# Linear attention on one core: Q of eight groups in 8 KB runs, with transposes and outputs taken by pairs of groups

## The chip, the cores and the metric

The kernel runs on one core of a Trainium2 chip. The metric is the device time of one execution in microseconds (us); lower is better. Each kernel was run several times beside the kernel before on the same chip. A ratio is the mean time of one kernel's fast runs over the mean of the other's fast runs of the same rounds, so it is not quite the ratio of the medians that are quoted. A run is called slow here when it lies more than 1.5% above the fastest run of the same kernel. With one core there is no second die to compare with, and for the changed kernel this limit cuts through one broad scatter (132.4 to 136.5 us), whose cause is looked at below.

The diffs are shortened, and some comments in them are not in the kernels. "Full" and "half clock" are read from the PEclk row of the profile (9 or 5 tenths granted) and from the times: the same 32 matmuls took 2.34 us and 4.48 us. PSUM is the memory in which the kernel keeps TensorE's results, SBUF the one for everything else on the chip that it works on.

The engines are TensorE (PE in the profile; PEld is its weight load), VectorE (DVE), ScalarE (ACT), GpSimd (POOL, which here issues most transfers) and SyncE (SP, which issues five).

## The reference

```python
batch, heads, seq, dim = 8, 12, 512, 64          # Q, K, V: float32
Q_feat = np.maximum(0, Q) + 1
K_feat = np.maximum(0, K) + 1
KV = np.einsum('bhkd,bhkv->bhdv', K_feat, V)
K_sum = np.sum(K_feat, axis=2)
numerator = np.einsum('bhqd,bhdv->bhqv', Q_feat, KV)
denominator = np.einsum('bhqd,bhd->bhq', Q_feat, K_sum)
return numerator / (denominator[:, :, :, None] + 1e-10)
```

Each of the 96 heads has 512 rows of 64. The three inputs are 37.7 MB and the output is 12.6 MB.

## The kernel before

The work is cut into 12 groups of 8 heads, two quads of four heads each. Pairs of groups share a load. A load casts fp32 to bf16 on its way. For each group VectorE makes the features of K and Q and spreads three quarters of V into a block layout (ScalarE the fourth); TensorE multiplies keys by values (`keys_values`), ScalarE brings the result (`kva`) from PSUM to SBUF; TensorE transposes Q's features into PSUM, ScalarE copies them out as `qt`; TensorE multiplies `qt` by `kva` (`output`), and VectorE divides out of PSUM into `o_sb`, which is stored. In the timelines of these runs each engine takes its instructions in the order of the program's calls: in group 9 of the changed kernel, output products that were ready began only at 97.45, when the transposes called before them were done.

```python
psum_qt = ctx.enter_context(tc.tile_pool(name="psum_qt", bufs=2, space=bass.MemoryType.PSUM))
...
def load(s, groups, names="kvq"):                  # 4 KB runs of fp32 per partition
    ...
        nc.gpsimd.dma_start(out=t[:, ms], in_=drams[x][:, 2 * groups[0] : 2 * groups[-1] + 2])

def load_pair(s):
    if s < NG // 2 - 1:
        load(s, (2 * s, 2 * s + 1))
    else:                                          # the last pair: by group
        load(s, (2 * s,))
        load(s, (2 * s + 1,))

def transposes(g):
    qf = qfs.pop(g)
    qt = mid_pool.tile([P, C, P, 2], BF16, name="qt")
    for half in range(2):
        qt_ps = psum_qt.tile([P, C, P], BF16, name="qt_ps")
        for c in range(C):
            nc.tensor.transpose(qt_ps[:, c, :], qf[:, half * C + c, :, :], identity)
        nc.scalar.copy(out=qt[:, :, :, half], in_=qt_ps)
    qts[g] = qt
...
for g in range(NG - 1):
    k_features(g)
    v_blocks(g)
    q_features(g)
    if g:
        transposes(g - 1)
    if g >= 2:
        output(g - 2)
    keys_values(g)
    if g % 2 and g // 2 + 2 < NG // 2:
        load_pair(g // 2 + 2)
    if g >= LAG:
        store(g - LAG)
last = NG - 1
k_features(last)
v_blocks(last)
transposes(last - 1)
output(last - 2)
q_features(last)
keys_values(last)
transposes(last)
output(last - 1)
output(last)
...
```

## Time and profile before

| | before |
|---|---|
| median of the first 3 runs | 127.46 us |
| span in the profile | 125.8 us |
| DMA | busy nine tenths or more in every slice from the second to the last but one |
| VectorE | 70% busy; its last instruction ends at 120.36 |
| VectorE idle ahead of reciprocals (first instruction of each output eviction) | 4.9 us in all |
| keys-by-values products, 32 matmuls of a group | 2.34 us at full clock, up to 4.48 at half |

The page of the profile has the span in 40 slices of some 3.1 us; a digit is the busy share in tenths, and the GB/s row counts a casting load by the bf16 that it writes, so 210 there is 420 of fp32 read. The groups list, for instructions of one line and tile, the busy time and the mean in ns, and behind the second bar how long the engine was idle ahead of them and what ended most of that. This is the row that the argument turns on, for the kernel before:

```profile
L199 DVE RECIPROCAL recip<-o_ps 128x8 f32<-128x8 f32 x48 | 9.6, 199 | 4.9 <-PE o_ps L189 4.8
```

VectorE waits for output products 4.8 us in the whole kernel.

### The profile page before, as it was taken

What the parts mean: (1) busy time and instruction counts of PE and PEld (TensorE: products, weight loads), DVE (VectorE), ACT (ScalarE), POOL (GpSimd) and SP (SyncE); (2) the same over time, 40 slices, a digit from 0 to 9 for tenths busy, and PEclk for the clock granted to TensorE, in tenths of its full rate; (3) what the DMA queues carried; (4) which work ended last, traced back from release to release, by engine and by line L of the source; (5) the groups of instructions that cost most, each with busy time, mean ns of one, the idle gap of its engine ahead of it and who ended that gap; (6) DMA issues with size and microseconds to landing.
All of it is one profiled execution on the core that took longest, in us unless ns stands there. A gap on an engine that the chain in (4) does not pass through costs nothing.

```text
span 125.8 us, 2337 instructions
## 1 busy us (share of the span) xinstructions
PE 65.2 (52%) x960; PEld 48.4 (39%) x960; DVE 88.2 (70%) x188; ACT 68.0 (54%) x87; POOL 27.8 (22%) x43
## 2 busy tenths in 40 slices
PE   0005939000059784796918476006978569694500
PEld 0003627000036564574806365004656447472300
DVE  4896280206199799999989990629959999758920
ACT  7832296006700889629892962750087971987000
POOL 6990213000002082023700260212221002020000
PEclk9999999755555999689999999955589976999955
DMA  3999999999999999999999999999999999999991
GB/s 76 341 211 209 210 213 211 210 212 211 212 211 212 211 214 212 210 212 214 253 414 287 209 210 212 213 369 380 209 210 210 211 287 418 418 417 410 403 391 72
DMA packets 13419, 32.13 MB, mean 255 GB/s; under 512 B 608, under 2 KB 608, under 8 KB 13408
## 3 DMA queue, kind: packets, MB, share of 16 engines
q0 software_dynamic: 12048, 28.84, 98.3%
q1 hardware_dynamic: 1360, 3.15, 6.8%
q8 instruction: 7, 0.11, 0.3%
q14 instruction: 4, 0.03, 0.1%
HBM read 37.75 MB, written 12.58 MB: 400 GB/s over the span
## 4 chain that ended last, share of the span: by engine, by line
DMA 40%; DVE 26%; PE 18%; POOL 6%; issue 6%; DVEq 0%; POOLq 0%
DMA q_raw<-in_Q_dram 40%; DVE o_sb L200 15%; PE kva_ps L157 11%; DVE v_all L140 4%; PE qt_ps L176 3%; DVE recip L199 3%; PE o_ps L189 3%; POOL v_raw L99 2%; DVE qf L122 2%; DVE kf L122 2%; POOL q_raw L99 1%; POOL kva_diag L231 1%; POOL k_raw L99 1%; POOL identity masks.py:199 0%; POOL identity masks.py:197 0%
## 5 line engine op out<-in xcount | busy, mean ns | idle before, releaser
L157 PE MATMUL kva_ps<-v_all,kf 128*64 128x320 bf16 x384 | 36.4, 356 | 13.1 <-DVE v_all L140 13.1
L189 PE MATMUL o_ps<-kva_diag,qt 128*64 128x130 bf16 x384 | 19.1, 234 | 40.9 <-DVE o_sb L200 40.4
L200 DVE TENSOR_TENSOR o_sb<-o_ps,recip 128x512 f32<-128x512 f32 x48 | 33.2, 692 | 1.6
L140 DVE COPY v_all<-v_raw 32x2048 bf16<-32x2048 bf16 x36 | 26.5, 736 | 10.9 <-DMA v_raw<-in_V_dram 10.6
L157 PEld LDWEIGHTS <-kf 128*64 128x64 bf16 x384 | 25.3, 133 | 20.9 <-DVE v_all L140 13.3
L189 PEld LDWEIGHTS <-qt 128*64 128x64 bf16 x384 | 12.7, 114 | 46.4 <-DVE o_sb L200 44.6
L138 ACT COPY v_all<-v_raw 32x2048 bf16<-32x2048 bf16 x12 | 22.7, 1894 | 13.3 <-DMA v_raw<-in_V_dram 13.1
L177 ACT COPY qt<-qt_ps 128x1024 bf16<-128x1024 bf16 x24 | 29.7, 1308 | 0.3
L167 ACT CAST kva_diag<-kva_ps 64x256 bf16<-64x256 f32 x24 | 8.9, 371 | 33.3 <-PE kva_ps L157 33.2
L122 DVE TENSOR_SCALAR qf<-q_raw 128x1024 bf16<-128x1024 bf16 x24 | 9.1, 423 | 6.6 <-DMA q_raw<-in_Q_dram 6.5
L99 POOL DMA_DIRECT2D k_raw<-in_K_dram x7 | 5.3, 754 | 38.1 <-DVE kf L122 37.3
L116 POOL DMA_DIRECT2D out_dram<-o_sb x10 | 8.4, 846 | 22.6 <-DVE o_sb L200 16.4
L176 PE MATMUL qt_ps<-identity,qf 128*128 128x128 bf16 x192 | 13.1, 222 | 0.0
L199 DVE RECIPROCAL recip<-o_ps 128x8 f32<-128x8 f32 x48 | 9.6, 199 | 4.9 <-PE o_ps L189 4.8
L122 DVE TENSOR_SCALAR kf<-k_raw 128x1024 bf16<-128x1024 bf16 x22 | 8.7, 437 | 6.0 <-DMA k_raw<-in_K_dram 6.0
L176 PEld LDWEIGHTS <-qf 128*128 128x128 bf16 x192 | 11.0, 99 | 3.3 <-issue 3.0
L99 POOL DMA_DIRECT2D v_raw<-in_V_dram x8 | 6.1, 764 | 18.8 <-ACT v_all L138 10.7
L99 POOL DMA_DIRECT2D q_raw<-in_Q_dram x8 | 5.9, 741 | 4.2 <-DMA q_raw<-in_Q_dram 4.2
L213 DVE MEMSET v_all<- 128x3072 f32 (+1 forms) x2 | 4.4, 2192 | 1.1 <-DVE ones L225 0.7
L168 ACT CAST kva_diag<-kva_ps 64x4 bf16<-64x4 f32 x24 | 4.0, 169 | 0.0
L214 ACT COPY v_all<-zero 128x2048 f32<-128x2048 f32 x2 | 3.7, 1894 | 0.0
L214 ACT ACT_TABLE_LOAD x1 | 1.3, 1283 | 0.7 <-PEq L273 0.7
(12 smaller groups left out, 4.6 us busy)
## 6 DMA issues: line engine op xcount, KB each, us to landing
out_dram<-o_sb POOLq DMA_DIRECT2D x10, 1024.0 KB, 20.2
k_raw<-in_K_dram POOLq DMA_DIRECT2D x4, 1024.0 KB, 18.0
v_raw<-in_V_dram POOLq DMA_DIRECT2D x4, 1024.0 KB, 20.9
q_raw<-in_Q_dram POOLq DMA_DIRECT2D x4, 1024.0 KB, 25.0
v_raw<-in_V_dram POOLq DMA_DIRECT2D x4, 512.0 KB, 17.3
q_raw<-in_Q_dram POOLq DMA_DIRECT2D x4, 512.0 KB, 17.1
out_dram<-o_sb SPq DMA_DIRECT2D x4, 512.0 KB, 5.1
k_raw<-in_K_dram POOLq DMA_DIRECT2D x3, 512.0 KB, 23.3
```

The source lines that it names most:

```text
L99: nc.gpsimd.dma_start(out=t[:, ms], in_=drams[x][:, 2 * groups[0] : 2 * groups[-1] + 2])
L116: nc.gpsimd.dma_start(out=o_to, in_=o_sb)
L122: nc.vector.tensor_scalar(out=dst, in0=src, scalar1=1.0, scalar2=1.0, op0=ALU.add, op1=ALU.max)
L138: nc.scalar.copy(out=v_blk[g % 2][ps, b], in_=v_raw[ps])
L140: nc.vector.tensor_copy(out=v_blk[g % 2][ps, b], in_=v_raw[ps])
L157: nc.tensor.matmul(kva_ps[64 * n : 64 * n + 64], lhsT=kf[:, c, n, :], rhs=vb[:, :, n, c, :], start=(c == 0), stop=(c == C2 - 1),)
L167: nc.scalar.copy(out=kva[ps, :, n, 0:D], in_=kva_ps[ps, sb : sb + 4, :])
L176: nc.tensor.transpose(qt_ps[:, c, :], qf[:, half * C + c, :, :], identity)
L177: nc.scalar.copy(out=qt[:, :, :, half], in_=qt_ps)
L189: nc.tensor.matmul(ops[c // 4][64 * j : 64 * j + 64, c // 2 % 2, (c % 2) * W : (c % 2) * W + W], lhsT=qt[:, c, 32 * b : 32 * b + 32, :], r ...
L199: nc.vector.reciprocal(out=recip, in_=cells[:, :, :, :, D:D1])
L200: nc.vector.tensor_tensor(out=o_sb[:, h:NP:2, 4 * i : 4 * i + 4].rearrange("p n (b c) d -> p b c n d", b=2), in0=cells[:, :, :, :, 0:D], i ...
```

## The change

Groups 2 to 9 read Q in 8 KB runs of fp32 per partition instead of 4 KB (a load is of sixteen heads in both kernels). A partition then holds rows of both groups' heads in another order, so a group's transposes give `qt` for parts of both groups, the outputs of a pair need the `qt` and the `kva` of both, and the transposes of a pair are made together. The store of each group goes to every second pair of heads. Two things come along: K and V of the last pair are one load each instead of one by group, and the calls at the end stand in another order. The idea is that longer runs cost the transfers less.

```diff
+    def eights(g):
+        return 2 <= g < NG - 2
+    def load_q(s):
+        t = in_pool.tile([P, 4, C2, D], BF16, name="q_raw").rearrange(
+            "p (n r) (q c) d -> p n (r q c) d", n=2, c=C)
+        nc.gpsimd.dma_start(out=t, in_=q_eights[:, 2 * s : 2 * s + 2])
     ...
     def load_pair(s):
-        if s < NG // 2 - 1:
-            load(s, (2 * s, 2 * s + 1))
-        else:
-            load(s, (2 * s,))
-            load(s, (2 * s + 1,))
+        pair = (2 * s, 2 * s + 1)
+        load("k", pair)
+        load("v", pair)
+        if eights(2 * s):
+            load_q(s)
+        else:
+            for g in pair:
+                load("q", (g,))
     ...
     def transposes(g):
-            nc.scalar.copy(out=qt[:, :, :, half], in_=qt_ps)
+            nc.scalar.copy(
+                out=qts[g][:, lo : lo + CC // 2], in_=qt_ps.rearrange("p c r q -> p c q r"))
     ...
     def output(g):
+                    if eights(g):
+                        b = 2 * (g % 2) + j
+                        kva = kva_diag[(g // 2 * 2 + h) % NV]        # NV: 4 instead of 3
+                        q = slice(16 * (4 * h + b), 16 * (4 * h + b) + 16)
     ...
-        for g in range(NG - 1):
+        for g in range(last):
             k_features(g)
             v_blocks(g)
-            q_features(g)
-            if g:
+            if not eights(g) and g < last - 1:
+                q_features(g)
+            if eights(g) and g % 2:
+                transposes(g - 1)
+                transposes(g)
+            elif g and not eights(g - 1):
                 transposes(g - 1)
             if g >= 2:
                 output(g - 2)
+            if eights(g) and g % 2 == 0:
+                q_features(g)
+                q_features(g + 1)
             keys_values(g)
     ...
         k_features(last)
         v_blocks(last)
+        output(last - 2)
+        keys_values(last)
+        q_features(last - 1)
         transposes(last - 1)
-        output(last - 2)
         q_features(last)
-        keys_values(last)
         transposes(last)
         output(last - 1)
         output(last)
```

More of the change, by code (lines that the diff above doesn't have):

```diff
@@ L44 @@
     C2 = 2 * C
+    C4 = 4 * C
     NPAIR = B * H * S // (P * C)
@@ L54 @@
     q_dram = view(Q, C2)
+    q_eights = view(Q, C4)
     k_dram = view(K, C2)
@@ L61 @@
     in_pool = ctx.enter_context(tc.tile_pool(name="in_pool", bufs=IN_BUFS))
-    feat_pool = ctx.enter_context(tc.tile_pool(name="feat", bufs=2))
-    mid_pool = ctx.enter_context(tc.tile_pool(name="mid", bufs=3))
+    kf_pool = ctx.enter_context(tc.tile_pool(name="kf_pool", bufs=2))
+    qf_pool = ctx.enter_context(tc.tile_pool(name="qf_pool", bufs=3))
+    mid_pool = ctx.enter_context(tc.tile_pool(name="mid", bufs=2))
     out_pool = ctx.enter_context(tc.tile_pool(name="out_pool", bufs=OUT_BUFS))
@@ L70 @@
     identity = const.tile([P, P], BF16, name="identity")
-    NV = 3
+    NV = 4
     v_all = const.tile([P, 9, 2, C2, D], BF16, name="v_all")
@@ L79 @@
     raw = {}
+    bufs = {}
     kfs = {}
@@ L83 @@
     outs = {}
+    def eights(g):
+        return 2 <= g < NG - 2
     def own(g):
-        return slice(g % 2 * 2, g % 2 * 2 + 2)
+        return slice(g % 2, 4, 2) if eights(g) else slice(g % 2 * 2, g % 2 * 2 + 2)
     def load_first_k():
@@ L91, in load_first_k, with load @@
         raw["k", 0] = k_raw
-    def load(s, groups, names="kvq"):
+    def load(x, groups):
+        s = groups[0] // 2
+        if groups[0] % 2 == 0 or (x, s) not in bufs:
+            bufs[x, s] = in_pool.tile([P, 4, C2, D], BF16, name=f"{x}_raw")
         ms = slice(groups[0] % 2 * 2, groups[-1] % 2 * 2 + 2)
-        for x in names:
-            if (x, "buf", s) not in raw:
-                raw[x, "buf", s] = in_pool.tile([P, 4, C2, D], BF16, name=f"{x}_raw")
-            t = raw[x, "buf", s]
-            nc.gpsimd.dma_start(
-                out=t[:, ms], in_=drams[x][:, 2 * groups[0] : 2 * groups[-1] + 2]
-            )
-            for g in groups:
-                raw[x, g] = t[:, own(g)]
-    def load_pair(s):
-        if s < NG // 2 - 1:
-            load(s, (2 * s, 2 * s + 1))
-        else:
-            load(s, (2 * s,))
-            load(s, (2 * s + 1,))
+        nc.gpsimd.dma_start(
+            out=bufs[x, s][:, ms], in_=drams[x][:, 2 * groups[0] : 2 * groups[-1] + 2]
+        )
+        for g in groups:
+            raw[x, g] = bufs[x, s][:, own(g)]
+    def load_q(s):
+        t = in_pool.tile([P, 4, C2, D], BF16, name="q_raw").rearrange(
+            "p (n r) (q c) d -> p n (r q c) d", n=2, c=C
+        )
+        nc.gpsimd.dma_start(out=t, in_=q_eights[:, 2 * s : 2 * s + 2])
+        rows = t.rearrange("p n (r c) d -> p n r c d", c=C)
+        for e in range(2):
+            raw["q", 2 * s + e] = rows[:, :, :, 4 * e : 4 * e + 4]
+    def load_pair(s):
+        pair = (2 * s, 2 * s + 1)
[3 more added lines that the diff above has]
+            load_q(s)
+        else:
+            for g in pair:
+                load("q", (g,))
     def store(g):
         o_sb = outs.pop(g)
-        o_to = o_dram[:, g * NP : g * NP + NP]
+        first = 2 * NP * (g // 2)
+        o_to = o_dram[:, first + g % 2 : first + 2 * NP : 2] if eights(g) else o_dram[
+            :, g * NP : g * NP + NP
+        ]
         if g < NG - 2:
@@ L127, in k_features @@
         k_raw = raw.pop(("k", g))
-        kf = feat_pool.tile([P, C2, 2, D], BF16, name="kf")
+        kf = kf_pool.tile([P, C2, 2, D], BF16, name="kf")
         for n in range(2):
@@ L143, in q_features @@
         q_raw = raw.pop(("q", g))
-        qf = feat_pool.tile([P, C2, 2, D], BF16, name="qf")
-        for half in range(2):
-            cs = slice(half * C, half * C + C)
-            feature(qf[:, cs].rearrange("p c n d -> p n c d"), q_raw[:, :, cs])
+        if not eights(g):
+            q_raw = q_raw.rearrange("p n (r c) d -> p n r c d", c=C)
+        R, CC = q_raw.shape[2:4]
+        qf = qf_pool.tile([P, R, CC, 2, D], BF16, name="qf")
+        for n in range(2):
+            feature(qf[:, :, :, n], q_raw[:, n])
         qfs[g] = qf
@@ L171, in transposes @@
         qf = qfs.pop(g)
-        qt = mid_pool.tile([P, C, P, 2], BF16, name="qt")
-        for half in range(2):
-            qt_ps = psum_qt.tile([P, C, P], BF16, name="qt_ps")
-            for c in range(C):
-                nc.tensor.transpose(qt_ps[:, c, :], qf[:, half * C + c, :, :], identity)
-            nc.scalar.copy(out=qt[:, :, :, half], in_=qt_ps)
-        qts[g] = qt
+        R, CC = qf.shape[1:3]
+        if R == 4 and g % 2:
+            qts[g] = qts[g - 1]
+        else:
+            qts[g] = mid_pool.tile([P, C, P, R], BF16, name=f"qt{R}")
+        first = g % 2 * CC if R == 4 else 0
+        for half in range(2):
+            qt_ps = psum_qt.tile([P, CC // 2, R, P], BF16, name="qt_ps")
+            for c in range(CC // 2):
+                for r in range(R):
+                    nc.tensor.transpose(
+                        qt_ps[:, c, r], qf[:, r, half * CC // 2 + c, :, :], identity
+                    )
+            lo = first + half * CC // 2
+            nc.scalar.copy(
+                out=qts[g][:, lo : lo + CC // 2], in_=qt_ps.rearrange("p c r q -> p c q r")
+            )
     def output(g):
-        kva = kva_diag[g % NV]
         qt = qts.pop(g)
@@ L187, in output @@
                 for j in range(2):
-                    b = 2 * h + j
+                    if eights(g):
+                        b = 2 * (g % 2) + j
+                        kva = kva_diag[(g // 2 * 2 + h) % NV]
+                        q = slice(16 * (4 * h + b), 16 * (4 * h + b) + 16)
+                    else:
+                        b = 2 * h + j
+                        kva = kva_diag[g % NV]
+                        q = slice(32 * b, 32 * b + 32)
                     nc.tensor.matmul(
                         ops[c // 4][64 * j : 64 * j + 64, c // 2 % 2, (c % 2) * W : (c % 2) * W + W],
-                        lhsT=qt[:, c, 32 * b : 32 * b + 32, :],
+                        lhsT=qt[:, c, q, :],
                         rhs=kva[:, b],
@@ L220 @@
         load_first_k()
-        load(0, (0,), "vq")
-        load(0, (1,))
+        load("v", (0,))
+        load("q", (0,))
+        for x in "kvq":
+            load(x, (1,))
         nc.vector.memset(ones, 0.0)
@@ L233 @@
         clear(5, 7, 9)
-        for g in range(NG - 1):
+        last = NG - 1
+        for g in range(last):
             k_features(g)
             v_blocks(g)
-            q_features(g)
-            if g:
+            if not eights(g) and g < last - 1:
[4 more added lines that the diff above has]
+            elif g and not eights(g - 1):
                 transposes(g - 1)
@@ L246 @@
                 store(g - LAG)
-        last = NG - 1
         k_features(last)
         v_blocks(last)
+        output(last - 2)
+        keys_values(last)
+        q_features(last - 1)
         transposes(last - 1)
-        output(last - 2)
         q_features(last)
-        keys_values(last)
         transposes(last)
```

## The prediction

> **What bounds the kernel now.** I read the page first (slices, queues, groups), then the timelines of VectorE, ScalarE and TensorE through an odd group and through the end, because the built program shows that the change reorders engines there.
>
> ```profile
> PE   0005939000059784796918476006978569694500
> DVE  4896280206199799999989990629959999758920
> PEclk9999999755555999689999999955589976999955
> DMA  3999999999999999999999999999999999999991
> GB/s 76 341 211 209 210 213 211 210 212 211 212 211 212 211 214 212 210 212 214 253 414 287 209 210 212 213 369 380 209 210 210 211 287 418 418 417 410 403 391 72
> ...
> q0 software_dynamic: 12048, 28.84, 98.3%
> ...
> L157 PE MATMUL kva_ps<-v_all,kf 128*64 128x320 bf16 x384 | 36.4, 356 | 13.1 <-DVE v_all L140 13.1
> L177 ACT COPY qt<-qt_ps 128x1024 bf16<-128x1024 bf16 x24 | 29.7, 1308 | 0.3
> ```
>
> The DMA row is full from the second slice to the last but one. About 210 GB/s are bf16 written by loads, so 420 GB/s of fp32 read; stores run at 417. Both directions at 420: 50.3 MB in 120 us. The kernel is bound by its transfers, and VectorE, at 70%, trails the loads and then the stores. Loads stop in the 34th slice, near 104.3 us; pure stores (418 GB/s) fill the rest.
>
> The margin of the compute is small at the end, as VectorE's last lines show. The last store can be issued at 120.4, and the span ends at 125.8.
>
> ```profile
> 119.44 0.20 DVE L199 RECIPROCAL recip<-o_ps 128x8 f32<-128x8 f32 x1
> 119.67 0.69 DVE L200 TENSOR_TENSOR o_sb<-o_ps,recip 128x512 f32<-128x512 f32 x1
> ```
>
> The same timeline in an odd group, 9, all engines: columns are start, duration, what, and the idle time before.
>
> ```profile
> 87.03 4.48 PE L157 MATMUL kva_ps<-v_all,kf 128*64 128x320 bf16 x32
> ...
> 91.44 1.36 PE L176 MATMUL qt_ps<-identity,qf 128*128 128x128 bf16 x16
> 91.55 0.37 ACT L167 CAST kva_diag<-kva_ps 64x256 bf16<-64x256 f32 x1 [7.96 <-PE kva_ps L157]
> ...
> 92.47 1.89 ACT L138 COPY v_all<-v_raw 32x2048 bf16<-32x2048 bf16 x1
> 92.73 0.48 PEld L189 LDWEIGHTS <-qt 128*64 128x64 bf16 x16
> 92.73 0.64 PE L189 MATMUL o_ps<-kva_diag,qt 128*64 128x130 bf16 x16
> ...
> 93.19 0.21 DVE L199 RECIPROCAL recip<-o_ps 128x8 f32<-128x8 f32 x1 [1.35 <-PE o_ps L189]
> ...
> 94.38 2.48 ACT L177 COPY qt<-qt_ps 128x1024 bf16<-128x1024 bf16 x2
> ```
>
> What to see: group 8's key-value products end at 91.5, the 16 transposes fill the two PSUM buffers, and the output products follow at once, 1.2 us after the products' end. ScalarE's three jobs (kva casts, its quarter of V, two qt copies) come after and hold nobody up.
>
> **What the Trainium skill says.** "DMA: Bandwidth & Descriptors", section "Where 436 GB/s comes from", puts the ceiling at 435 GB/s; 420 here is 96.5% of it. The same page, "Why small descriptors are slow (HBM only)", gives a fixed overhead per packet and per descriptor; longer runs can save only what lies between 420 and 435. "TensorE: Matmul & The Clock Gate", "What's actually happening": the array runs at half clock by default and activity over some 3.4 us releases it. The trace agrees: the clock row falls to 5 where PE is idle, and 32 key-value products take 4.48 us at 87.03 but 2.34 us at 95.27, when it is granted fully. "ScalarE: Activation LUTs", "What ACT_TABLE_LOAD costs", gives 186 ns + 0.833 ns an element. The 2048-element V copies agree (1894 ns), the qt copies do not: 1308 ns for 1024 elements, where the formula gives 1039. They write every second bf16 of qt. "Advanced Engine Details and Errata", "Memory Cachelines", has a penalty for accesses that hop from line to line (8 bytes in PSUM); nothing in this trace shows it for ScalarE's reads, and the new copy reads PSUM that way.
>
> **The change part by part.**
> 1. Q in 8 KB runs. 4 KB at 420/16 GB/s an engine is 156 ns; at 435/16, 150.6. So at most 5.4 ns a packet are overhead. Groups 2 to 9 have 8 x 256 = 2048 Q packets, 128 an engine; half of them go: 64 x 5.4 ns = 0.35 us saved on a transfer-bound kernel. Bytes, stores (2 KB runs) and load order are otherwise as before.
> 2. Q features of both groups of a pair move to the even group, behind its output. VectorE need no longer sit before that output until the pair's Q lands (2.88 us at 34.26, 2.77 at 84.10). Same number of instructions, 0.42 us each.
> 3. Transposes of both groups stand in the odd group, ahead of output(g-2) on TensorE: 32 instead of 16 with the same two PSUM buffers. The second 16 wait for ScalarE's first two copies, and these stand behind the kva casts and the V copy. From the end of the products to output's first eviction it was 1.0 + 0.4 = 1.4 us at full clock (measured 1.7 at half). Now: casts 0.92 + V copy 1.89 + two qt copies 2.5 + 0.5 (half the transposes) + 0.4 (first output products) = 6.2 us. That is 4.8 us more on the path of VectorE, four times over. VectorE has only 3.1 us of K and V work (4.5 with Q) to lay over it.
> 4. Output of an even group now needs the kva of both its groups, so also the odd group's products just before it: products 2.34 + casts 0.92 + first output 0.4 against VectorE's 2.8 us of K and V work. About covered at full clock, 1.5 to 2 us short at half.
> 5. The last pair's K and V come as one transfer each, so V of group 10 lands with V of group 11. Loads end near 104.3, the two Q halves are the last 2 x 2.5 us, so V lands near 99.3 instead of about 94. VectorE began those copies at 97.2 before: 2 us later at best.
> 6. Transposes 10 and 11 both come after keys_values(11); before, those of 10 lay two outputs earlier.
>
> Cadence of a pair on VectorE: output odd 3.36 + K and V 2.85 + output even 3.36 + (products 2.34 - 1.3, since they start when the last output products of the group have gone, + 6.2) = 16.8 us. With one of the two sets of products at half clock (some 4 us, as five of ten were at least partly slow before) 18.3. VectorE's plain work is 14.0 (two groups at 0.75 + 2.2 + 0.76 + 3.36). The transfers allow 15 us a pair early and 20 where stores join, so VectorE falls behind at first and recovers later. Output 1 starts near 42.2 and output 7 after three more pairs: 42.2 + 50.4 = 92.6 at full clock, 97.1 otherwise (93.2 before).
>
> Tail: K of group 10 done at 96.7 or 101.2. From the later of that and 99.3: V 2.2, output(8) 3.36, K and V of 11 2.85, output(9) 3.36, then products -1.3 + 2.34, casts 0.92, two copies 2.5, half the transposes and first products 0.9 (5.4 together), outputs 10 and 11 6.7 = 23.9 us. VectorE ends at 123.2, or at 125.1, or at 126.6 if keys_values(11) is also cold (before: 120.4). After that the last 0.5 MB store: 5.4 us before, behind a backlog; without one some 4.1, an estimate from the 1 MB first K, which landed in 5.0, less 1.25 for half the bytes, plus 0.4 to the end of the span. Span 127.3 to 130.7; the time was 1.7 over the span (127.54 against 125.8): 129.0 to 132.4. I take 130.8, the cold case weighing a little more than the warm, because TensorE now idles some 4 us in every odd group.
>
> **Rivals.**
> - *The transfers stay the bound.* The queue never empties, stores wait in it, and every delay of VectorE is absorbed. Then only the 0.35 us of step 1 counts: 127.1. For it: the DMA row, and VectorE's 30% idle. Against it: the last store already is issued 5.4 us before the end, of which some 4 cannot shrink, so there is room for hardly 1.5 us.
> - *The new qt copy changes its price.* It writes qt contiguously and reads PSUM with a 256-byte step. If the second-element write was what cost 270 ns, it falls to about 1.04 us: 0.5 us less in each odd group and in the tail, some 1 to 2.5 in all, so 128.5 to 130. If the hopping read costs, at 1.6 to 1.9 us a copy, four of them a pair: 133 to 136.
> - *Outputs no longer held by Q are the gain.* VectorE starts output(0) at 31.3 instead of 35, and could run ahead. Against it: it is then stopped in the same pair by step 3, which costs more than the 2.8 us won.
>
> **Range and chances.** 80% range 127.6 to 134.8: below is the transfer-bound case, above the slow copy with cold products. Slower by over 2% begins at 130.0. Warm and cheap copies fall below it, cold ones or dear copies above: slower 0.57, same 0.39, faster 0.04, the last because step 1 offers a quarter of a per cent.
>
> **What would show it.** Right: in groups 3, 5, 7, 9 VectorE idles 3 to 5 us before a reciprocal, released by output products, and TensorE's transposes wait for ScalarE's qt copies; VectorE's last instruction ends at 122 to 127; the final slices show GB/s below 400 as the queue runs dry; the software queue has about 1,024 packets fewer. Wrong: VectorE ends by 120.5 with the DMA row full to the end; or copies of about 1.0 us; or a load rate well above 420 GB/s in the Q stretches, which would make step 1 worth more than I give it.

## The result, and the profile after

| | before | changed |
|---|---|---|
| median | 127.26 us (4 runs, 126.75 to 127.83) | 133.67 us (4 runs, 132.38 to 135.21) |
| ratio of the fast runs | 1 | 1.041 (95%: 1.033 to 1.049) |
| span profiled | 125.8 us | 130.6 us |
| VectorE starts K features of group 10 | 96.56 | 101.51 |
| VectorE's last instruction ends | 120.36 | 126.38 |
| from there to the end of the span | 5.4 us | 4.2 us |
| software DMA packets | 12,048 | 10,992 |

The change is slower by 4.1%, by the two of its four runs that the 1.5% limit leaves; the mean of all four, 133.73 us, is 5.1% above that of before. The prediction said 130.8 us with a range of 127.6 to 134.8, and slower as the likelier outcome. The rows of the page of the changed kernel that answer to those of before:

```profile
PE   0006968001982897754795917958376569566530
DVE  4895460209990497990799952999909999953960
PEclk9999999965577556998559995599968967999755
DMA  2999999999999999999999999999999999963474
GB/s 100 321 211 210 212 210 209 210 218 207 211 213 215 219 208 209 213 216 221 403 319 210 212 216 213 374 361 213 212 211 211 346 418 419 410 266 149 186 300 156
...
L183 PE MATMUL kva_ps<-v_all,kf 128*64 128x320 bf16 x384 | 38.2, 368 | 12.9 <-DVE v_all L164 10.9
...
L241 DVE RECIPROCAL recip<-o_ps 128x8 f32<-128x8 f32 x48 | 9.6, 200 | 20.4 <-PE o_ps L231 20.2
L212 ACT COPY qt<-qt_ps 128x1024 bf16<-128x1024 bf16 x24 | 23.1, 1016 | 0.8 <-PE qt_ps L208 0.4
```

Three things are to be seen. First, the DMA row is as full as before until the 35th slice and then breaks: 266, 149, 186 GB/s. The loads have landed by then; what is left are stores, which wait for results. Before, they were the bound to the last slice; now VectorE sets the end. Second, the reciprocal row: VectorE waits 20.2 us for output products where it waited 4.8. Third, single slices where Q comes show 213 to 221 GB/s, but slices next to them fall to 207 to 209: over slices 3 to 18, which hold loads alone, the mean is 211.9 against 211.3 before. If the longer runs give anything, it is little.

Where the 20 us are is seen in VectorE's timeline: lines that begin with a wait for output products. Columns are start, duration, what, and the idle time before.

```profile
44.30 0.21 DVE L241 RECIPROCAL recip<-o_ps 128x8 f32<-128x8 f32 x1 [5.37 <-PE o_ps L231]
51.40 0.21 DVE L241 RECIPROCAL recip<-o_ps 128x8 f32<-128x8 f32 x1 [0.70 <-PE o_ps L231]
62.78 0.21 DVE L241 RECIPROCAL recip<-o_ps 128x8 f32<-128x8 f32 x1 [3.69 <-PE o_ps L231]
80.66 0.21 DVE L241 RECIPROCAL recip<-o_ps 128x8 f32<-128x8 f32 x1 [3.75 <-PE o_ps L231]
98.14 0.21 DVE L241 RECIPROCAL recip<-o_ps 128x8 f32<-128x8 f32 x1 [3.33 <-PE o_ps L231]
119.48 0.21 DVE L241 RECIPROCAL recip<-o_ps 128x8 f32<-128x8 f32 x1 [3.40 <-PE o_ps L231]
```

They are the odd groups 3, 5, 7 and 9, a small one in group 4, and one in the tail. Group 9, TensorE and ScalarE:

```profile
89.30 2.36 PE L183 MATMUL kva_ps<-v_all,kf 128*64 128x320 bf16 x32
...
91.59 1.07 PE L208 MATMUL qt_ps<-identity,qf 128*128 128x128 bf16 x16
91.70 0.37 ACT L193 CAST kva_diag<-kva_ps 64x256 bf16<-64x256 f32 x1 [2.45 <-PE kva_ps L183]
...
92.62 1.89 ACT L162 COPY v_all<-v_raw 32x2048 bf16<-32x2048 bf16 x1
...
94.53 1.93 ACT L212 COPY qt<-qt_ps 128x1024 bf16<-128x1024 bf16 x2
95.60 1.92 PE L208 MATMUL qt_ps<-identity,qf 128*128 128x128 bf16 x16 [2.94 <-ACT qt L212]
...
97.45 1.07 PE L231 MATMUL o_ps<-kva_diag,qt 128*64 128x130 bf16 x16
```

Read it against group 9 of before in the prediction. The first 16 transposes are done at 92.7 and fill both PSUM buffers. The second 16 start at 95.60, when ScalarE has cast `kva`, copied its quarter of V and copied the first `qt` buffer. The output products, which need none of this (their `qt` was ready long before), stand behind them in TensorE's order and start at 97.45. From the end of the products at 91.66 to VectorE's reciprocal at 98.14 it is 6.5 us; before it was 1.7.

The sum of the loss on VectorE: 4.95 us later at group 10 (101.51 against 96.56), and 1.07 us more from there to the end (24.87 against 23.80). Of these 6.0 us the end of the span shows 4.8, because the last store, with the queue empty, takes 4.2 us and not 5.4.

### The profile page after: what moved, and what is told of

The parts are those of the page before. It is cut to its first block, busy times and chain, and to the rows that moved or that the text cites. A ratio compares the mean times of both kernels' runs of the same rounds, so it can differ in the third digit from the quotient of the medians.

```text
span 130.6 us, 2339 instructions
## 1 busy us (share of the span) xinstructions
PE 74.3 (57%) x960; PEld 57.6 (44%) x960; DVE 88.8 (68%) x188; ACT 61.4 (47%) x87; POOL 26.4 (20%) x42
## 3 DMA queue, kind: packets, MB, share of 16 engines
q0 software_dynamic: 10992, 28.84, 93.6%
## 4 chain that ended last, share of the span: by engine, by line
DVE 27%; PE 26%; ACT 19%; DMA 15%; POOL 5%; issue 4%; ACTq 0%; DVEq 0%; POOLq 0%
PE kva_ps L183 16%; DVE o_sb L242 16%; DMA v_raw<-in_V_dram 15%; ACT v_all L162 9%; ACT qt L212 6%; DVE v_all L164 6%; PE qt_ps L208 5%; PE o_ps L231 4%; DVE recip L241 4%; ACT kva_diag L193 4%; POOL kva_diag L275 2%; DVE kf L146 2%; POOL v_raw L108 1%; POOL q_raw L108 1%; ACT kva_diag L194 1%
## 5 line engine op out<-in xcount | busy, mean ns | idle before, releaser
L183 PE MATMUL kva_ps<-v_all,kf 128*64 128x320 bf16 x384 | 38.2, 368 | 12.9 <-DVE v_all L164 10.9
L183 PEld LDWEIGHTS <-kf 128*64 128x64 bf16 x384 | 28.3, 138 | 19.9 <-DVE v_all L164 11.8
L231 PE MATMUL o_ps<-kva_diag,qt 128*64 128x130 bf16 x384 | 22.6, 264 | 24.6 <-DVE o_sb L242 17.7
L231 PEld LDWEIGHTS <-qt 128*64 128x64 bf16 x384 | 16.0, 133 | 30.9 <-DVE o_sb L242 22.1
L162 ACT COPY v_all<-v_raw 32x2048 bf16<-32x2048 bf16 x12 | 22.7, 1893 | 10.0 <-DMA v_raw<-in_V_dram 9.8
L208 PE MATMUL qt_ps<-identity,qf 128*128 128x128 bf16 x192 | 16.6, 249 | 13.6 <-ACT qt L212 13.4
L241 DVE RECIPROCAL recip<-o_ps 128x8 f32<-128x8 f32 x48 | 9.6, 200 | 20.4 <-PE o_ps L231 20.2
L212 ACT COPY qt<-qt_ps 128x1024 bf16<-128x1024 bf16 x24 | 23.1, 1016 | 0.8 <-PE qt_ps L208 0.4
L208 PEld LDWEIGHTS <-qf 128*128 128x128 bf16 x192 | 13.9, 112 | 16.8 <-issue 16.1
L140 POOL DMA_DIRECT2D out_dram<-o_sb x10 | 7.7, 767 | 40.9 <-DVE o_sb L242 40.9
L108 POOL DMA_DIRECT2D k_raw<-in_K_dram x6 | 4.7, 777 | 36.7 <-DVE kf L146 36.7
L108 POOL DMA_DIRECT2D v_raw<-in_V_dram x7 | 5.4, 765 | 10.9 <-ACT v_all L162 10.4
## 6 DMA issues: line engine op xcount, KB each, us to landing
k_raw<-in_K_dram POOLq DMA_DIRECT2D x5, 1024.0 KB, 16.8
```

The lines of the kernel that those rows point to most:

```text
L108: nc.gpsimd.dma_start(out=bufs[x, s][:, ms], in_=drams[x][:, 2 * groups[0] : 2 * groups[-1] + 2])
L140: nc.gpsimd.dma_start(out=o_to, in_=o_sb)
L162: nc.scalar.copy(out=v_blk[g % 2][ps, b], in_=v_raw[ps])
L183: nc.tensor.matmul(kva_ps[64 * n : 64 * n + 64], lhsT=kf[:, c, n, :], rhs=vb[:, :, n, c, :], start=(c == 0), stop=(c == C2 - 1),)
L208: nc.tensor.transpose(qt_ps[:, c, r], qf[:, r, half * CC // 2 + c, :, :], identity)
L212: nc.scalar.copy(out=qts[g][:, lo : lo + CC // 2], in_=qt_ps.rearrange("p c r q -> p c q r"))
```

## The experiments

All results were right but one. In the tables below "waits" is the idle time of VectorE ahead of reciprocals over the whole kernel, from the page's groups.

### The second group's transposes behind the output

```diff
             if eights(g) and g % 2:
                 transposes(g - 1)
-                transposes(g)
             ...
             if g >= 2:
                 output(g - 2)
+            if eights(g) and g % 2:
+                transposes(g)
```

> The changed kernel with one edit: in the odd groups the second group's transposes stand behind the older output, so that only one group's 16 transposes stand ahead of it, as before. Theory (TensorE holds the output back behind ScalarE's casts, V copy and qt copies): the waits of 3.3 to 5.4 us before the odd groups' outputs shrink to under 1.5 us, VectorE keeps up with the transfers until the last pair's V lands near 99.3, ends near 122.5, and the time falls from 132.5 to about 128.3 (127.5 to 129.3). Rival (the last pair's coarser loads and the order of the end make the loss): the waits go but the time stays above 131. Rival (the half clock makes it): 131 or more, with the odd groups' products still at 3.5 us and more.

Measured: 129.72 us median (128.95 to 131.46), ratio 1.016 (1.011 to 1.021). The rows of this run: the reciprocals' group, and the lines of the end of VectorE's loop.

```profile
L241 DVE RECIPROCAL recip<-o_ps 128x8 f32<-128x8 f32 x48 | 9.6, 200 | 4.7 <-PE o_ps L231 4.4
```

```profile
99.07 2.08 DVE L164 COPY v_all<-v_raw 32x2048 bf16<-32x2048 bf16 x3 [4.32 <-DMA v_raw<-in_V_dram]
...
117.12 0.21 DVE L241 RECIPROCAL recip<-o_ps 128x8 f32<-128x8 f32 x1 [3.69 <-PE o_ps L231]
```

No wait of the outputs in groups 3, 5, 7 and 9 is left; of the 4.7 us, 3.69 and 0.72 are in the tail. VectorE has caught up with the transfers and now waits 4.3 us for the V of the last pair, which lands at 99.07. The time is 0.4 us above the range expected, and VectorE ends at 123.9 and not 122.5: group 10's products ran at half clock (4.47 us), which gave the wait of 0.72 us; the rest of the difference was not traced. Moving 16 transposes in each pair takes the loss from 4.1% to 1.6%. The half clock does not make the waits: the products that stand just ahead of the odd groups' outputs, those of groups 2, 4, 6 and 8, took 3.77, 2.36, 3.68 and 4.32 us here and 4.28, 2.36, 2.36 and 2.36 in the changed kernel, and the waits are gone all the same. The products of the odd groups themselves did run at full clock here (2.36 us each; 4.47, 3.87, 3.47 and 2.34 in the changed kernel), so part of the 3.0 us between the fast runs' means may be the clock's.

### The order of the end as before

```diff
-            if not eights(g) and g < last - 1:
+            if not eights(g):
                 q_features(g)
 ...
+        transposes(last - 1)
         output(last - 2)
-        keys_values(last)
-        q_features(last - 1)
-        transposes(last - 1)
         q_features(last)
+        keys_values(last)
         transposes(last)
```

> The changed kernel with the order of the end as before: Q features of group 10 in the loop, its transposes ahead of output 9. Theory: the waits of the odd groups stay at 3.3 to 5.4 us, only the one of 3.4 us at 119.5 shrinks to 1.0 to 1.7; gain 1.5 to 2.5 us, time 130 to 131. Rival (the end is all of the loss): below 128.5. Rival (the end costs nothing): 132 or more.

Measured: 132.05 us (131.13 to 133.02), ratio 1.037 (1.030 to 1.044). In the tail the theory is borne out: the wait of 3.40 us is 1.69 now, and from K features of group 10 to VectorE's end it is 22.7 us instead of 24.9. The time gained less than expected, because this run came to group 10 later, at 103.12 against 101.51. Its groups 4 and 5 had both their products at half clock (4.04 and 4.48 us). The gain of the order is 2.2 us in this stretch; what the odd groups lose scatters by nearly as much. By the time alone nothing is shown: 132.05 is outside the 130 to 131 expected and meets the sign of the rival that the end costs nothing, and the interval overlaps that of the change.

### The last pair's K and V by group

```diff
     def load_pair(s):
         ...
-        load("k", pair)
-        load("v", pair)
         if eights(2 * s):
+            load("k", pair)
+            load("v", pair)
             load_q(s)
         else:
             for g in pair:
-                load("q", (g,))
+                for x in "kvq":
+                    load(x, (g,))
```

> The changed kernel with the last pair's K and V loaded by group again and nothing else. Theory: VectorE reaches group 10 at 101.5, after both V have landed, so the earlier landing (near 94) is of no use: 132 to 135, as the change. Rival (the coarse loads are part of the loss by themselves): 131 or less.

Measured: 134.77 us (134.38 to 134.97), ratio 1.057 (1.051 to 1.063), no gain. The runs lie in the upper part of the changed kernel's scatter, so nothing is to be read into their being above its median. Undoing this part alone gains nothing, because VectorE is late anyway: it came to group 10 at 103.2, after both V had landed.

### All three undone, and two of three

The next kernels combine the edits above. Everything else of the change (8 KB runs, outputs by pairs of both quads, stores) stays.

> The changed kernel with the second transposes behind, the order of the end as before and the last pair's K and V loaded by group again; 8 KB runs of Q, outputs by pairs of heads and stores are as in the change. Theory: the whole loss is undone and the 0.35 us of the longer runs are left: 126.4 to 127.4, same as before or 0.3 us faster, and the DMA row full to the end. Rival (outputs by pairs of both quads, which wait for the odd group's kva, cost something too): 128 to 130, with VectorE waiting ahead of even outputs.

> The changed kernel with the second transposes behind the output and the order of the end as before, but the last pair's K and V still in one load each. Sum: V lands at 99.1 (seen with the transposes behind alone), copies 2.1, Q features 0.8, output 8 3.4, K and V of 11 3.0, output 9 3.4, Q features 0.7, wait 1.7, outputs 10 and 11 6.7: VectorE ends at 120.8, its last store lands 4.2 later at 125.0, just inside the transfers' end of 125.2. Time 126.8 to 127.6, against 128.9 to 129.9 for the transposes alone. If the coarse loads bind by themselves: 128.3 or more.

> The changed kernel with the second transposes behind the output and the last loads by group, but the new order of the end. Sum from the run of all three, where V of 11 is copied by 103.7: output 9 3.4, Q features of both groups 1.4, wait 3.5, outputs 6.7: VectorE ends at 118.7, well inside the transfers' end. Time 126.7 to 127.5. If the order of the end binds by itself: 128.3 or more.

| kernel | median, us | ratio (95%) | waits, us | VectorE ends | span |
|---|---|---|---|---|---|
| second transposes behind | 129.72 | 1.016 (1.011 to 1.021) | 4.7 | 123.9 | 128.2 |
| and the end as before | 128.45 | 1.007 (1.000 to 1.014) | 3.5 | 122.0 | 126.2 |
| and last loads by group, the end as changed | 126.70 | 0.996 (0.991 to 1.001) | 7.8 | 120.3 | 124.9 |
| all three | 126.91 | 0.9957 (0.992 to 0.999) | 2.3 | 116.3 | 125.2 |

With all three, VectorE is done at 116.3, 4 us earlier than in the kernel before, and the span is still 125.2. The page of that run shows why:

```profile
DMA  3999999999999999999999999999999999999993
GB/s 73 339 211 211 211 210 208 212 215 213 210 211 212 217 215 207 211 214 218 237 412 309 195 210 217 217 336 402 215 208 213 211 251 416 421 410 412 416 402 136
```

The transfers are the bound again from end to end, and compute that ends 4 us earlier is worth nothing. That version is faster than the kernel before by 0.4%, with an interval just clear of 1. The outputs across both quads cost nothing that can be seen: the rival of 128 to 130 us is out.

The run with the end as before but coarse loads missed its expectation (126.8 to 127.6) by about 1 us. The wait for V was there as foreseen (4.58 us, until 99.24), but group 10's products took 3.41 us, partly at half clock, which gave a wait of 0.60 us more ahead of output 9, and Q of group 10 was waited for another 0.37. VectorE ended at 122.0 instead of 120.8, and the span at 126.2, 4.2 later. So the coarse loads do bind by themselves once nothing else does, by about a microsecond, 0.6 of it through the half clock; the new order of the end, with loads by group, does not: VectorE ends at 120.3, at the edge, and the transfers set the end.

### The kernel before with Q in 8 KB runs

The Q loads of groups 2 to 9 alone are read in 8 KB runs; the values land in other rows, so the result is wrong (relative error 0.025).

```diff
+            if x == "q" and len(groups) == 2:
+                nc.gpsimd.dma_start(
+                    out=t.rearrange("p (n r) c d -> p n (r c) d", n=2),
+                    in_=q_eights[:, 2 * s : 2 * s + 2])
+            else:
                 nc.gpsimd.dma_start(out=t[:, ms], in_=drams[x][...])
```

> The kernel before with the four paired Q loads read in 8 KB runs and nothing else changed; the result is wrong on purpose, as the values land in other rows. It measures step 1 alone. Theory: 1,024 software packets fewer, about 324 ns each instead of two of 156 by issue rate, and 0.2 to 0.5 us less: 126.7 to 127.2. Rival (long runs are much better): 125.5 or less. Rival (they are worse): 128 or more.

Measured: 127.07 us (126.88 to 127.75), ratio 0.998 (0.994 to 1.002), and 11,024 software packets, 1,024 fewer. The mean gain is 0.28 us, where 0.35 was worked out, but the interval holds 1: whether it is real can't be said from these six runs. By the interval it is not more than about 0.8 us. If it is real, the intent of the change is worth a fifth of a per cent. (The 324 ns a packet in the expectation do not fit its own sum: two of 156 are 312, and 5.4 less is some 307.)

### The kernel before with the transposes together

The reverse test: the old kernel with the one thing that was found to hurt.

```diff
-            if g:
+            if 3 <= g < 10 and g % 2:
+                transposes(g - 1)
+                transposes(g)
+            elif 0 < g < 3 or g > 10:
                 transposes(g - 1)
```

> The kernel before with one thing of the change: in groups 3, 5, 7 and 9 the transposes of both groups of the pair stand ahead of the older output, and the even groups have none; 4 KB runs, outputs, loads, stores and the end are as before. Theory: the same wait appears without any other part of the change; VectorE waits 3 to 5 us for output products in each odd group (1.35 us at most before), ends between 121.5 and 124.5 instead of 120.4, and the time is 128.3 to 131. Rival (the wait needs the pairing of outputs, the 8 KB layout or the new copy): 127 to 127.8.

Measured: 136.74 us in the one fast run, 143.1, 143.2 and 152.4 in slow ones. The profile fell on the slowest: all products took 4.7 to 4.9 us, half clock from the first to the last, and the page has no clock row.

> The kernel before with both groups' transposes ahead of the older output, again, because the first look fell on a run with TensorE at half clock throughout (products 4.7 to 4.9 us). Runs of the first time: 136.7 fast, 143 and 152 slow. Theory: 134 to 138 in a fast run, with waits of 3.5 to 5.5 us in the odd groups; more than the change's 132.5 because its qt copies take 1.31 us each instead of 1.01 and Q features still stand ahead of the output. Rival (the earlier look was the slow state alone): under 131.

Measured: 139.80 us (136.83 to 141.54), fast runs 136.83 and 138.46, ratio 1.080 (1.072 to 1.089). In the profile of a fast run VectorE waits 24.0 us ahead of reciprocals:

```profile
L199 DVE RECIPROCAL recip<-o_ps 128x8 f32<-128x8 f32 x48 | 9.6, 200 | 24.0 <-PE o_ps L189 23.9
```

The order of the transposes needs no other part of the change to do its harm. The first expectation was right in kind and far too small: 128.3 to 131, with VectorE's end at 124.5 at the latest, where it ended at 133.0. The output in group 3 started at 48.67, after a wait of 6.67 us, and from there a pair took 18.5 to 19 us. The harm is larger than in the changed kernel: VectorE came to group 10 at 108.6, the change at 101.5. The qt copies stay at 1,307 ns (1,016 there), Q is still waited for (2.89 us at 34.19), and the products of groups 2 to 11 took 34.1 us (31.3 there); what each of these adds was not measured apart.

### ScalarE's V copy behind the qt copies

```diff
+            if b == 3 and eights(g) and g % 2:
+                late[g] = (v_blk[g % 2][ps, b], v_raw[ps])
-            if b == 3:
+            elif b == 3:
                 nc.scalar.copy(out=v_blk[g % 2][ps, b], in_=v_raw[ps])
 ...
                 transposes(g - 1)
                 transposes(g)
+                dst, src = late.pop(g)
+                nc.scalar.copy(out=dst, in_=src)
```

> The changed kernel with ScalarE's V copy of groups 3, 5, 7 and 9 behind its four qt copies instead of ahead of them. Theory (the output is held by ScalarE's queue): VectorE's waits in the odd groups shrink by the 1.9 us of that copy, from 3.3 to 3.7 to 1.4 to 2.0; the group's products then wait 0.8 us for V, so some 1.0 us a pair are won: 130 to 132, against 132.5. Rival (held by the transposes themselves or by TensorE's clock): the waits stay above 3 us.

Measured: 130.29 us (129.77 to 131.24), ratio 1.023 (1.018 to 1.029). The waits of the odd groups:

```profile
40.81 0.21 DVE L244 RECIPROCAL recip<-o_ps 128x8 f32<-128x8 f32 x1 [1.93 <-PE o_ps L234]
57.39 0.21 DVE L244 RECIPROCAL recip<-o_ps 128x8 f32<-128x8 f32 x1 [2.30 <-PE o_ps L234]
73.01 0.21 DVE L244 RECIPROCAL recip<-o_ps 128x8 f32<-128x8 f32 x1 [1.23 <-PE o_ps L234]
...
91.37 0.21 DVE L244 RECIPROCAL recip<-o_ps 128x8 f32<-128x8 f32 x1 [2.29 <-PE o_ps L234]
```

Their mean is 1.94 us, against 4.04 in the changed kernel: 2.1 us less for a copy of 1.89. Nothing on TensorE or VectorE was touched, so it is ScalarE's queue that holds the output back, through the two PSUM buffers. The clock does not explain it: the products just ahead of these outputs took 3.38, 3.80, 2.36 and 3.95 us here, no less than the 4.28, 2.36, 2.36 and 2.36 of the changed kernel in sum, and all products were slower (mean matmul 397 ns against 368). It was faster all the same.

### The changed kernel again, and TensorE kept busy

> The changed kernel once more, on the same chip as the next three: 132 to 135, VectorE ending at 126 to 129. What differs between its runs should be the half clock: the runs with a lower granted clock are the longer ones.

> The changed kernel with 32 more matmuls in each odd group, placed in TensorE's wait between the first and the second 16 transposes; they write the PSUM tile that the group's own products overwrite, so the result stays right. Theory: part of the loss is the half clock that TensorE falls to in that wait; kept busy, the odd groups' products take 2.3 to 2.6 us instead of 3.5 to 4.5, the waits of VectorE stay near 3 us, group 10 is reached by 98, its V is waited for until 99.1, VectorE ends near 123.5 and the time is 129 to 130.5. Rival (the clock is a symptom and costs nothing): as the change. Rival (more matmuls only add work): slower than the change.

```diff
                 transposes(g - 1)
+                # 32 matmuls of kf into the PSUM tile that keys_values(g) starts over
+                ...                            # kva_next[g] and some are made here
+                for c in range(C2):
+                    for n in range(2):
+                        nc.tensor.matmul(kva_next[g][...], lhsT=kf[:, c, n, :], rhs=some,
+                                         start=(c == 0), stop=(c == C2 - 1))
                 transposes(g)
```

The changed kernel again: 135.02 us (132.79 to 136.45); the profile fell on the longest run, whose VectorE ended at 130.5, later than the 126 to 129 expected. By mean granted clock the runs do not line up (132.79 at 0.801, 134.96 at 0.800, 136.45 at 0.781), so that expectation is not borne out as it was put. What does go with the time is the clock in the products. Over groups 2 to 11 they took 35.4 us in this run and 31.3 in the first profile, 4.1 us apart, and the two runs are 136.45 and 132.38, also 4.1 apart. One of the two is a slow run, on another chip. The run with the last loads by group, a fast one whose edit gained nothing, lies between: 34.5 us of products and 134.97 us. Three runs agree with the products' clock going into the time; they do not prove it.

With TensorE kept busy: 132.76 us (129.67 to 133.76). In the odd groups the products took 2.34 us each, as expected, and the waits of VectorE in these groups stayed:

```profile
43.96 0.21 DVE L244 RECIPROCAL recip<-o_ps 128x8 f32<-128x8 f32 x1 [4.93 <-PE o_ps L234]
62.00 0.21 DVE L244 RECIPROCAL recip<-o_ps 128x8 f32<-128x8 f32 x1 [3.92 <-PE o_ps L234]
78.70 0.21 DVE L244 RECIPROCAL recip<-o_ps 128x8 f32<-128x8 f32 x1 [2.58 <-PE o_ps L234]
96.30 0.21 DVE L244 RECIPROCAL recip<-o_ps 128x8 f32<-128x8 f32 x1 [3.67 <-PE o_ps L234]
```

In group 9 all of TensorE's work from the transposes on ran at full clock (16 transposes in 1.22 us instead of 1.92), and the wait is 3.67 us, no less than the 3.33 of the changed kernel. So the waits do not come from the clock. What the clock adds to the time is less sure. The mean of all four runs is 132.2 against 134.8 for the changed kernel on the same chip, and the one fast run of each is 129.67 against 132.79. That would put some 2.6 to 3.1 us on the clock, but three of four runs on each side are slow ones and with one fast run on each side there is no interval, and the profiled run was not at its best: the products of group 11 at the end took 4.48 us, and VectorE ended at 126.7. The expectation of 129 to 130.5 holds for one run of four. What the half clock alone costs is left as an estimate.

## Why the prediction was right, point by point

**What bounds.** Right. Before, the transfers; the margin of the compute at the end was taken as hardly 1.5 us, and the run whose VectorE ended at 122.0 (1.7 later than before) had a span of 126.2, 0.4 longer. From there every microsecond counts: in the five profiles with VectorE's end between 122.0 and 126.4 that were looked at for this, the span ends 4.2 to 4.3 us later, where 4.1 was estimated.

**Step 1, 8 KB runs, 0.35 us.** Right in size as far as it can be seen: 0.28, not clear of zero. The ceiling of 435 GB/s that the working takes is, by its page, one of the SBUF ports, and on that side a casting load moves 210 GB/s here; that it limits the fp32 read is an assumption.

**Step 2, Q features behind the even output.** Right: the waits of 2.9 and 2.8 us for Q are gone (0.3 in all), and output 0 began at 31.2, where 31.3 was worked out. In the changed kernel it bought nothing that shows: the wait of 5.37 us in group 3 follows.

**Step 3, the transposes together.** Right, and the main cause: 2.5 of the 4.1 points go with moving 16 transposes in each pair, and the reverse test on the old kernel gives 8%. The 6.2 us from the end of the products to the first eviction measured 6.5, but two terms were mis-sized and cancelled, which was luck. The two qt copies took 1.93 us instead of 2.5; the second 16 transposes and the first output products ran at half clock and took some 1.7 us where 0.9 was allowed. "Five of ten" sets of products at half clock before is a misreading: of groups 2 to 11 four took more than 2.34 us (4.16, 3.55, 4.48, 4.01). From one odd group's output to the next it was 18.5, 17.9 and 17.5 us, close to the 18.3 worked out with one cold set of products (16.8 warm); VectorE's plain work of a pair adds up to 14.1, not 14.0.

**Step 4, even outputs wait for both kva.** Small: one wait of 0.7 us in group 4. "1.5 to 2 us short at half" was too much.

**Step 5, coarse loads of the last pair.** The landing was right to 0.3 us (99.3 predicted, 99.07 seen). In the changed kernel itself it costs nothing, since VectorE is there only at 101.5; it binds once step 3 is mended, by 1 us (end as before) to 2 points (end as changed).

**Step 6, the order of the end.** Right: 5.4 us from output 9's end to output 10 were worked out and 5.1 were measured; undoing it took 2.2 us off the tail, though not off the time beyond the noise.

**The sum.** The cold case of the prediction had K of group 10 done at 101.2 and VectorE at its end at 125.1 to 126.6; measured were 102.3 and 126.4. The point of 130.8 was 1.7 us under the 132.5 of the fast runs (2.9 under the median of all four); it mixed in a warm case that did not occur: in neither profile of the changed kernel did all odd groups run at full clock. The rival of cheaper qt copies was half right. They did become cheaper, 1.01 us, which the prediction had named as a sign of being wrong, and the time did not fall to 128.5 to 130. That the half clock took back what they gave fits the terms of step 3; no run tests it alone. The other signs came as named: waits of 3.3 to 3.8 us in three odd groups (5.4 in group 3), VectorE's end at 126.4, slices under 400 GB/s at the end, and 1,056 packets fewer.

## What to carry to other kernels

In an engine that executes in order, ask of each instruction what it waits for and who stands behind it. Sixteen transposes that waited for another engine's queue held back products that were ready, and cost some ten times what the longer DMA runs gave, if these gave anything (2.5 points against 0.2). A change for the bound resource pays only if the others keep their slack: first work out how late the second engine may be (estimated here at 1.5 us; 1.7 us later made the span 0.4 us longer), then move work. Doubling a batch that goes through a buffer sized for one makes the second half wait for the drain; put independent work between the halves.

## What the Trainium skill lacked or had wrong

- "ScalarE: Activation LUTs", "What ACT_TABLE_LOAD costs": the formula (186 ns + 0.833 ns an element, 1,039 ns for 1,024) fits the new qt copy, which reads PSUM with a 256-byte step and writes in one piece (1,012 to 1,042 ns), but not the old one, which reads in one piece and writes every second bf16 (1,291 to 1,332 ns). The two copies differ in the reading and in the writing, and no run changes one alone; the page has no cost for either.
- "Advanced Engine Details and Errata", "Memory Cachelines": for PSUM the section says that scattered access slows matmuls, and nothing of ScalarE's reads. In these no penalty was seen; the copy that hops was the faster one, 1,016 against 1,308 ns in the mean.
- "TensorE: Matmul & The Clock Gate", "What's actually happening": the table there gives an idle window of some 3.4 us. In the kernel before, a pause of 2.06 us among thin output products (before 101.25) was followed by 32 products in 4.01 us, where 2.34 is full clock. The page's section "A second HAM failure mode: psum-queue depth-cycling" does say that frequent short pauses can throttle; how much activity in a window keeps the clock it does not say. Its remark that the clock records can't be fully trusted agrees with one run here, which recorded a mean of 1.0 while all products took 4.7 to 4.9 us.
- No page has what runs of 8 KB instead of 4 KB are worth in a casting load: here 0.28 us on 127, not clear of zero.
